# Fixed places in VectorE's queue for joins, combining and turned rows, and earlier pair sums, in a float32 encoder block with Strassen-like products

## The chip, the core and the metric

The kernel runs on one NeuronCore of one Trainium2 chip. The metric is the device time of one execution in microseconds. A core has five engines that run side by side and meet only at semaphores: TensorE (PE, the matmuls; PEld are its weight loads), VectorE (DVE), ScalarE (ACT), GpSimd (POOL) and SyncE (SP, which here issues the DMAs that bring weights in). TensorE writes its results into PSUM, eight banks in all; the kernel hands PSUM out in four tiles of two banks.

## What is computed

One layer of an encoder block on 256 rows of 2048 float32 values: half a SwiGLU feed-forward step, a mixer (causal pooling and gated linear attention), cross-attention to 256 memory rows, and a second feed-forward half step. Of the reference only this matters here:

```python
def swiglu(h, w_gate, w_up, w_down):
    return (jax.nn.silu(h @ w_gate) * (h @ w_up)) @ w_down

x = x + 0.5 * swiglu(rms_norm(x, ffn1_norm), ffn1_w_gate, ffn1_w_up, ffn1_w_down)
...                                   # mixer and cross-attention, which the change does not touch
x = x + 0.5 * swiglu(rms_norm(x, ffn2_norm), ffn2_w_gate, ffn2_w_up, ffn2_w_down)
out = rms_norm(x, final_norm)
```

The hidden width is 5632 = 11 x 512 columns.

## The kernel before, in words

**Precision by splitting.** Every float32 matrix is split into a high part (ScalarE: a copy rounded to fp32r, `wh`, `xh`) and a low part (VectorE: the source less the high part, `wl`, `xl`). A product is then three matmuls: high x high, high x low, low x high (`products`, L330).

**Weights' units.** All weights come in units of 1 MB (`raw`, 128 x 2048). A unit is loaded by one DMA, split, and multiplied. `Stream` (class at the head of the file) keeps a list of units and, between them, operations (`st.op(f, after)`: f is placed after so many further units). `emit` walks the list and splits weights two units ahead of the one being multiplied (`AHEAD = 2`; three `raw` buffers, three buffers each of `wh` and `wl`).

**Two kinds of units.** A plain unit (called p below) covers two k-tiles by 1024 columns: one high copy of 128 x 2048 on ScalarE, one low part of 128 x 2048 on VectorE (L248), 24 matmuls. A seven unit (called s; `split_seven`, `seven`) replaces eight block products by seven, in Winograd's manner: VectorE forms column sums `T` (three additions, L431), then the low part `xl` (128 x 1536, L248) and the low part `wl` of T (L435); ScalarE makes `xh` and two halves of `wh` (L434); TensorE has 21 matmuls (L456). The left operands of a seven unit are sums of pairs of activation tiles, made once for a feed-forward step by `Sums.make` (L387 to L399, four pairs: `x_sums`).

**A block** (`block_s`) is one pass over all 2048 rows of a weight for 1024 columns, in the order s0 p1 s2 p3 s4 s6 p5 p7. It uses all four PSUM tiles. Two hold the parts that only seven units feed (banks P1, P6 and P7, P5); the other two hold P2, P4 (called j=1) and P3, P0 (j=0). After the last seven unit, `combine` (L512 on ScalarE, L513, L514, L517 on VectorE) folds the first two tiles into an SBUF tile `sg` and so frees them. After p7, `join` (L527, twice: j=1, then j=0) adds the other two tiles to `sg` and frees those. The first unit of the next block first multiplies into its P1, P6, P7, P5 (12 matmuls) and then into P2, P4, P3.

**A feed-forward step** has its hidden columns in three parts of 4, 4 and 3 x 512 (`FF_PARTS`). Parts one and two run the blocks G1 (gate), U1 (up), G2, U2 and then the product with w_down. Part three runs G1, U1, one block `both` for the remaining gate and up columns, and w_down. The very first G1 of a step has no seven units (`block_t`); meanwhile `x_sums` is made. I call the change from U1 to G2 the early seam and that from G2 to U2 the late seam. After U1, `late_up` (L787) multiplies gate by up, and `turn` transposes the hidden rows into `ys` in the middle of the next block: 16 transposes into two PSUM tiles named `ph` (L797), a high copy on ScalarE (L253) and a low part on VectorE (L254). `CLEAR = 7` puts this after seven units of the next block, that is between its p5 and p7.

**What sets the order.** The program is not issued as written: a planner reorders the instructions of each engine by its own model of their times and by priorities, and hands out PSUM tiles as they come free in that plan. Only edges restrain it. `in_turn` chains every operation of the weights' splitting on VectorE and on ScalarE into one sequence. `among_weights(f)` inserts f's instructions into these two sequences: behind the newest splitting operation, ahead of the next. `behind_weights(f)` only keeps f behind. In the kernel before, `combine` in the feed-forward steps, `x_sums.make` and a few more are among the weights; `join` and the split in `turn` are not, so the planner puts them where it likes.

Of the kernel before, what the change touches and what calls it, by code (L numbers as in the profile page):

```python
# [90 lines left out]
def build(ctx, tc, I, out):  # L91
    nc = tc.nc
    st = Stream()
# [70 lines left out]
    sums = ctl("sums", [P, 2])  # L164
# [73 lines left out]
    def among_weights(f):  # L238


        scalar, vector = behind_weights(f)
        latest["vector"] = vector
        if scalar is not None:
            latest["scalar"] = scalar
# [7 lines left out]
    def split(hi, lo, src):  # L252
        high = nc.scalar.copy(hi, src)  # L253
        return high, nc.vector.tensor_tensor(out=lo, in0=src, in1=f32(hi), op=ALU.subtract)  # L254
# [202 lines left out]
                    banks[n], x, w, start=n in fresh and j == 0, stop=n in ends and j == 2  # L457
                )

    def block_s(srcs, act, sums, order, evict, merge=None, sevens=None):  # L460

        sevens = [g for g in order if g in (sevens or sums.pairs)]
        held, seen = {"banks": {}}, set()

        def banks(*names):
            t = ptile(uid("pt"))
            for i, n in enumerate(names):
                held["banks"][n] = t[:, i]  # L470
            return t

        def open_whole():
            if "ps" not in held:
                c = banks("P2", "P4")
                held["ps"] = (banks("P3", "P0"), c)

        def open_parts():
            held["parts"] = (banks("P1", "P6"), banks("P7", "P5"))

        names = {(1, 0): "P2", (1, 1): "P4", (0, 0): "P3", (0, 1): "P0"}

        def unit_s(g):
            def fn(weights):
                if g == sevens[0]:
                    open_parts()
                open_whole()
                fresh = {f"P{i}" for i in range(1, 8)} - seen
                seen.update(fresh)
                ends = ("P1", "P5", "P6", "P7") if g == sevens[-1] else ()  # L490
                seven(held["banks"], act, sums, g, fresh, ends, weights)
            return fn

        def unit_p(g):
            def fn(wh, wl):
                open_whole()
                wh, wl = (w.rearrange("p (k j n) -> p k j n", j=2, n=NB) for w in (wh, wl))
                for j in (1, 0):
                    for h in range(2):
                        n = names[j, h]  # L500
                        for kk in range(2):
                            products(held["banks"][n], act, 2 * g + kk, h, wh[:, kk, j],
                                     wl[:, kk, j], n not in seen and kk == 0,
                                     g == order[-1] and kk == 1)
                        seen.add(n)
            return fn

        def combine():

            e = held["e"] = scope["pool"].tile([P, 4, NB], F32, tag="sg", name=uid("sg"), bufs=2)  # L510
            a, b = held["parts"]
            nc.scalar.copy(e[:, 0], a[:, 0])  # L512
            nc.vector.tensor_tensor(out=e[:, 3], in0=a[:, 1], in1=e[:, 0], op=ALU.add)  # L513
            nc.vector.tensor_tensor(  # L514
                out=e[:, 1:3], in0=b, in1=e[:, 3:4].to_broadcast([P, 2, NB]), op=ALU.add
            )
            last = nc.vector.tensor_tensor(out=e[:, 3], in0=b[:, 1], in1=e[:, 1], op=ALU.add)  # L517
            if merge is not None:
                merge(e[:, 2:4], e[:, 0:2])
            return None, last  # L520

        def join(j):
            if merge is not None:
                evict(j, held["ps"][j])
                return
            e = held["e"][:, 0:2] if j else held["e"][:, 2:4]
            nc.vector.tensor_tensor(  # L527
                out=e, in0=held["ps"][j], in1=e, op=ALU.add if j else ALU.subtract
            )
            evict(j, e)  # L530

        for g in order:
            if g in sevens:
                st.unit(srcs[g], unit_s(g), split_seven)
                if g == sevens[-1]:
                    st.op(combine if merge else lambda: among_weights(combine))
            else:
                st.unit(srcs[g], unit_p(g))
        for j in (1, 0):
            st.op(lambda j=j: join(j))  # L540
# [35 lines left out]
    def wwide(w, n0, k0=0, nk=KT):  # L576

        def src(k):
            def load(raw):
                raw = raw.rearrange("p (k n) -> p k n", n=2 * NB)  # L580
                if len(loaded) < 3:
                    for kk in range(2):
                        parts = (0, NB) if not loaded else (0,)
                        for c in parts:
                            n = 2 * NB // len(parts)
                            wload(raw[:, kk : kk + 1, c : c + n], w, k + kk, 1, n0 + c, n)
                else:
                    wload(raw, w, k, 2, n0, 2 * NB)
                next(first_loads, None)
                loaded.append(1)  # L590
            return load
        return [src(k0 + k) for k in range(0, nk, 2)]
# [171 lines left out]
    def ffn(wg, wu, wd, down, amid=None):  # L764
        gate = {}
        x_sums = Sums("xe", xs, PAIRS, True)

        def hidden():
            e = scope["pool"].tile([P, 4, NB], F32, tag="sg", name=uid("sg"), bufs=2)
            return {0: e[:, 2:4], 1: e[:, 0:2]}  # L770

        def ev_gate(j, c, fresh):

            if fresh and fresh == 1 + j:
                gate["new"] = hidden()
            g = gate["new"][j] if fresh else c
            gate[j] = g
            for h in range(2):
                nc.scalar.activation(g[:, h, :], c[:, h, :], AF.Silu, scale=Rcol[:, h : h + 1])

        def late_up(held, j, c):
            behind_weights(lambda: ev_up(j, c, held))

        def ev_up(j, c, held=gate):
            g = held[j]
            for h in range(2):
                nc.vector.scalar_tensor_tensor(  # L787
                    out=g[:, h, :], in0=c[:, h, :], scalar=Rcol[:, h : h + 1], in1=g[:, h, :],
                    op0=ALU.mult, op1=ALU.mult,
                )  # L790

        def turn(g, k):

            v = four(ptile(uid("ph")))
            for i in range(4):
                for h in range(2):
                    nc.tensor.transpose(  # L797
                        v[:, i, h * P : (h + 1) * P], g[:, h, i * P : (i + 1) * P], ident
                    )
            split(ys[:, k : k + 4, 0, :], ys[:, k : k + 4, 1, :], v)  # L800

        for i, g in enumerate(PAIRS):
            st.op(lambda g=g: among_weights(lambda: x_sums.make(g)), (4, 7, 9, 10)[i])
        for lo, n in FF_PARTS:
            whole = n == KT // 4
            for b in range(0, n - 1, 2):
                n0 = (lo + b) * NB
                if lo == b == 0:
                    block_t(wwide(wg, n0), xs, lambda j, ps: ev_gate(j, ps, 1), amid=amid)
                else:  # L810
                    block_s(wwide(wg, n0), xs, x_sums, ORDER, lambda j, c: ev_gate(j, c, 0))
                held, up = {}, {}
                into_down = whole and b
                block_s(wwide(wu, n0), xs, x_sums, ORDER, up.__setitem__)
                st.op(lambda held=held: held.update(gate))
                for j in (1, 0):
                    st.op(lambda j=j, held=held, up=up: late_up(held, j, up[j]),
                          0 if into_down else 3)
                wait = 1 if into_down else CLEAR
                for j in range(2):  # L820
                    st.op(lambda j=j, b=b, held=held: turn(held[j], 4 * (b + j)), wait)
            if n % 2:
                def both(j, c):
                    if j:
                        ev_gate(1, c, 0)
                        gate[0] = gate[1]
                    else:
                        ev_up(0, c)
                block_s(wtwo(wu, wg, (lo + n - 1) * NB), xs, x_sums, ORDER, both)
                st.op(lambda n=n: turn(gate[0], 4 * (n - 1)), 1)  # L830
            if whole:
                make_y_sums()
            down(wd, 4 * lo, 4 * n, lo + n == FF // NB, y_sums if whole else None)
# [646 lines left out]
```

## Time and profile before

| what | us |
|---|---|
| median of 3 runs before (2124.1 to 2125.37) | 2124.6 |
| the profiled execution, its own time | 2124.74 |
| span of its trace, first to last instruction | 2122.9 |
| TensorE busy | 2095.6 |
| VectorE busy | 1705.0 |
| ScalarE busy | 1108.7 |
| DMA queues busy, share of 16 engines | 61% |
| granted TensorE clock, mean | 0.995 |

The rows quoted below have these forms. A timeline row: start, duration (us from the span's start), engine, line, operation, tile written <- tiles read, shapes, count, and in brackets the idle time of the engine ahead of it and what ended it. A row of the waits: who waited for whom, us in total, times, longest. A row of the chain (followed back from the last instruction): start, us, what. A row of the windows: the stretch, its length, then for PE, PEld, DVE, ACT and POOL the busy time and count, the granted clock, the DMA share and GB/s. Matmuls are pipelined: one of 512 columns shows about 0.39 us, while the next starts about 0.227 us after it.

### The profile page before, as it was taken

The numbers are of one execution on the slowest core, as the hardware profiler recorded it, in microseconds if no ns is written. First come the engines' busy times: TensorE is split into PE (matmuls) and PEld (weight loads), VectorE is DVE, ScalarE is ACT, GpSimd is POOL, SyncE is SP. The second block draws the span as 40 slices with busy tenths as digits, with TensorE's granted clock in tenths as the row PEclk, the third lists the DMA queues.
The fourth block names the chain that finished last, engine by engine and source line by source line (L and its number), as shares of the span: only waits on it lengthen the run. The fifth ranks groups of instructions, "written<-read, shape, count | busy, mean of one in ns | idle before, by whom it ended". The sixth has DMA issues, their size and how long they took to land.

```text
span 2122.9 us, 24500 instructions
## 1 busy us (share of the span) xinstructions
PE 2095.6 (99%) x9916; PEld 1748.2 (82%) x9916; DVE 1705.0 (80%) x1537; ACT 1108.7 (52%) x1084; POOL 14.3 (1%) x41
## 2 busy tenths in 40 slices
PE   9999999999999999999999999999999999999998
PEld 8778888788888888888888888888788887888876
DVE  6998899988997577688765546779988999889974
ACT  7554455544554545454645434456554555445544
POOL 0000000000000000000000000000000000000001
PEclk9999999999999999999999999999999999999999
DMA  7556666566656565467755555665567655676673
GB/s 268 187 196 213 246 204 208 185 218 237 218 198 241 198 199 181 157 198 243 252 179 175 163 172 165 198 231 185 198 218 236 220 190 191 214 242 213 201 256 118
DMA packets 143609, 435.95 MB, mean 205 GB/s; under 512 B 9860, under 2 KB 13544, under 8 KB 143112
## 3 DMA queue, kind: packets, MB, share of 16 engines
q1 hardware_dynamic: 143464, 434.38, 61.2%
q8 instruction: 78, 1.28, 0.2%
q14 instruction: 35, 0.29, 0.0%
q10 hardware_dynamic: 32, 0.01, 0.0%
HBM read 417.58 MB, written 16.78 MB: 205 GB/s over the span
## 4 chain that ended last, share of the span: by engine, by line
PE 82%; DVE 13%; issue 2%; ACT 1%; DMA 1%; SPq 0%; DVEq 0%; ACTq 0%
PE pt L330 39%; PE pt L456 15%; PE pa L315 15%; PE pb L330 6%; DVE wl L248 3%; PE pe L330 3%; DVE T L431 3%; DVE wl L435 2%; DVE xl L248 2%; DVE sg L527 1%; DVE sg L787 1%; PE pl L1215 1%; PE pv L1250 1%; PE ph L797 0%; PE px L718 0%
## 5 line engine op out<-in xcount | busy, mean ns | idle before, releaser
L248 DVE TENSOR_TENSOR wl<-raw,wh 128x2048 fp32r<-128x2048 f32 (+2 forms) x284 | 638.1, 2251 | 286.2 <-ACT wh L247 284.9
L247 ACT CAST wh<-raw 128x2048 fp32r<-128x2048 f32 (+2 forms) x284 | 532.6, 1880 | 408.4 <-PE pt L330 183.1
L330 PE MATMUL pt<-wh,xs 128*128 128x512 f32 x1536 | 495.0, 390 | 0.0
L330 PE MATMUL pt<-wh,ys 128*128 128x512 f32 x1440 | 449.2, 390 | 0.0
L434 ACT CAST wh<-T 128x1024 fp32r<-128x1024 f32 x196 | 205.7, 1053 | 331.2 <-DVE T L431 301.2
L330 PEld LDWEIGHTS pt<-wh,xs 128*128 128x128 f32 x1536 | 287.9, 188 | 59.3
L330 PEld LDWEIGHTS pt<-wh,ys 128*128 128x128 f32 x1440 | 269.9, 188 | 56.0 <-ACT wh L247 0.5
L315 PE MATMUL pa<-xs,wh 128*128 128x512 f32 x896 | 315.8, 397 | 0.0
L330 PE MATMUL pt<-wl,xs 128*128 128x512 f32 x768 | 300.0, 391 | 0.0
L330 PE MATMUL pt<-wl,ys 128*128 128x512 f32 x720 | 280.5, 390 | 0.0
L315 PE MATMUL pa<-xs,wl 128*128 128x256 f32 x896 | 248.3, 281 | 0.0
L435 DVE TENSOR_TENSOR wl<-T,wh 128x2048 fp32r<-128x2048 f32 x98 | 223.8, 2284 | 2.1 <-ACT wh L434 1.8
L315 PEld LDWEIGHTS pa<-xs,wh 128*128 128x128 f32 x896 | 167.6, 188 | 38.1 <-issue 0.3
L248 DVE TENSOR_TENSOR xl<-raw,xh 128x1536 fp32r<-128x1536 f32 x98 | 171.6, 1751 | 12.9 <-ACT xh L247 12.9
L315 PEld LDWEIGHTS pa<-xs,wl 128*128 128x128 f32 x896 | 169.1, 189 | 1.7 <-issue 0.2
L330 PEld LDWEIGHTS pt<-wl,xs 128*128 128x128 f32 x768 | 144.3, 188 | 30.0
L247 ACT CAST xh<-raw 128x1536 fp32r<-128x1536 f32 x98 | 144.9, 1479 | 27.7 <-PE pt L456 22.6
L330 PEld LDWEIGHTS pt<-wl,ys 128*128 128x128 f32 x720 | 135.2, 188 | 28.0
L431 DVE TENSOR_TENSOR T<-T,raw 128x512 f32<-128x512 f32 x196 | 135.3, 690 | 5.3
L456 PE MATMUL pt<-wh,xs 128*128 128x512 f32 x320 | 126.8, 396 | 7.6 <-DVE sg L527 7.6
L456 PE MATMUL pt<-wh,xe 128*128 128x512 f32 x320 | 124.6, 395 | 0.0
L456 PE MATMUL pt<-xh,xs 128*128 128x512 f32 x320 | 120.4, 396 | 2.5 <-DVE sg L527 2.5
(236 smaller groups left out, 2354.1 us busy)
## 6 DMA issues: line engine op xcount, KB each, us to landing
raw<-in_ffn_w_down SPq DMA_DIRECT2D x88, 1024.0 KB, 5.6
raw<-in_ffn_w_up SPq DMA_DIRECT2D x80, 1024.0 KB, 5.0
raw<-in_ffn_w_gate SPq DMA_DIRECT2D x77, 1024.0 KB, 5.0
raw<-in_w_in SPq DMA_DIRECT2D x32, 1024.0 KB, 5.2
raw<-in_xattn_w_kv SPq DMA_DIRECT2D x32, 1024.0 KB, 5.3
raw<-in_w_out SPq DMA_DIRECT2D x16, 1024.0 KB, 5.7
raw<-in_xattn_w_q SPq DMA_DIRECT2D x16, 1024.0 KB, 6.0
raw<-in_xattn_w_o SPq DMA_DIRECT2D x16, 1024.0 KB, 5.6
```

Source lines behind the costliest of these rows:

```text
L247: in_turn("scalar", lambda: nc.scalar.copy(hi, src))
L248: in_turn("vector", lambda: nc.vector.tensor_tensor(out=lo, in0=src, in1=f32(hi), op=ALU.subtract))
L315: nc.tensor.matmul(o, w, x, start=k == 0 and i == 0, stop=last and i == 1)
L330: nc.tensor.matmul(ps, a, w, start=first and i == 0, stop=last and i == 2)
L431: in_turn("vector", lambda: nc.vector.tensor_tensor(out=o, in0=a, in1=b, op=ALU.add))
L434: in_turn("scalar", lambda: nc.scalar.copy(th[:, c], t[:, c]))
L435: in_turn("vector", lambda: nc.vector.tensor_tensor(out=tl, in0=t, in1=f32(th), op=ALU.subtract))
L456: nc.tensor.matmul(banks[n], x, w, start=n in fresh and j == 0, stop=n in ends and j == 2)
L527: nc.vector.tensor_tensor(out=e, in0=held["ps"][j], in1=e, op=ALU.add if j else ALU.subtract)
L787: nc.vector.scalar_tensor_tensor(out=g[:, h, :], in0=c[:, h, :], scalar=Rcol[:, h : h + 1], in1=g[:, h, :], op0=ALU.mult, op1=ALU.mult,)
L1215: nc.tensor.matmul(ps[:, t, :M], ys[:, 4 * h + d, a, tok], xa["K"][:, d, b, :], start=i == 0, stop=i == 11,)
L1250: nc.tensor.matmul(ps[:, d, :S], xa["V"][:, m, a, col], xa["PT"][:, m, b, :], start=i == 0, stop=i == 5,)
```

## The change

Four edits, all about order; no instruction is added or removed.

1. `join` in the feed-forward blocks goes through `among_weights`: both joins of a block stand behind the low part of the next block's p1, and ahead of everything of its s2.
2. `combine` of the up blocks comes one unit later (`late=1`): behind the split of the next block's first unit (s0) instead of behind p7's.
3. The split of turned rows, where `turn` runs inside the next block (all b = 0), goes through `among_weights`: ScalarE's two copies and VectorE's two low parts stand behind s0's split and ahead of p1's.
4. `x_sums.make` for the four pairs comes after units 2, 4, 6, 8 of the first gate block instead of 4, 7, 9, 10.

```diff
-    def block_s(srcs, act, sums, order, evict, merge=None, sevens=None):
+    def block_s(srcs, act, sums, order, evict, merge=None, sevens=None, late=0):
...
-            nc.vector.tensor_tensor(
+            among_weights(lambda: (None, nc.vector.tensor_tensor(
                 out=e, in0=held["ps"][j], in1=e, op=ALU.add if j else ALU.subtract
-            )
+            )))
             evict(j, e)
...
-                    st.op(combine if merge else lambda: among_weights(combine))
+                    st.op(combine if merge else lambda: among_weights(combine), late)
...
-        def turn(g, k):
+        def turn(g, k, queued=False):
...
-            split(ys[:, k : k + 4, 0, :], ys[:, k : k + 4, 1, :], v)
+            parts = lambda: split(ys[:, k : k + 4, 0, :], ys[:, k : k + 4, 1, :], v)
+            among_weights(parts) if queued else parts()
...
-            st.op(lambda g=g: among_weights(lambda: x_sums.make(g)), (4, 7, 9, 10)[i])
+            st.op(lambda g=g: among_weights(lambda: x_sums.make(g)), (2, 4, 6, 8)[i])
...
-                block_s(wwide(wu, n0), xs, x_sums, ORDER, up.__setitem__)
+                block_s(wwide(wu, n0), xs, x_sums, ORDER, up.__setitem__, late=1)
...
-                    st.op(lambda j=j, b=b, held=held: turn(held[j], 4 * (b + j)), wait)
+                    st.op(lambda j=j, b=b, held=held, queued=not into_down: turn(
+                        held[j], 4 * (b + j), queued), wait)
```

## The prediction

> **What bounds the kernel now.** First the head of the page:
>
> ```profile
> span 2122.9 us, 24500 instructions
> PE 2095.6 (99%) x9916; PEld 1748.2 (82%) x9916; DVE 1705.0 (80%) x1537; ACT 1108.7 (52%) x1084; POOL 14.3 (1%) x41
> ```
>
> TensorE is the bound, and no edit takes work from it. A gain can only be time in which it stands. I therefore read what PE waited for over the whole span (the two largest rows), then in 740:1400 us, mixer and attention (last row):
>
> ```profile
> PE pt L456 <- DVE sg L527: 10.0, 4, 2.5
> PE pt L456 <- DVE xl L248: 4.5, 9, 1.4
> PE pt L456 <- DVE xl L248: 0.7, 2, 0.3
> ```
>
> Four times TensorE waits for a join and seven times (nine less two) in the feed-forward steps for a low part `xl`. One more wait, 1.4 for a turned row at the last w_down, has its row below. A matmul's shown end lies 0.16 us behind its slot (0.39 in the rows below, while the next starts after 0.23), so each wait costs 0.16 more than shown: joins 10.6, `xl` 3.8 + 7 x 0.16 = 4.9, turned row 1.6. Next, in the chain, what follows the four joins:
>
> ```profile
> 143.67 6.42 PE pt L456 x20
> 402.49 4.84 PE pt L456 x13
> 407.32 2.75 PE pt L330 x12
> 1535.42 4.83 PE pt L456 x13
> 1792.53 4.74 PE pt L456 x13
> ```
>
> Twelve matmuls in 2.75 us are 0.229 each; at that pace 20 take 4.6 and 13 take 3.0. After each wait TensorE runs slow for a while and loses another 6.42 - 4.6 = 1.8, and 1.8 to 1.9 at the others as well. The four places, all late seams, cost 10.6 + 7.3 = 17.9. With the `xl` waits and the turned row, **24.4 us** can go at most.
>
> Now the second late seam, VectorE's timeline, then rows of ScalarE's and TensorE's:
>
> ```profile
> 396.75 1.22 DVE L527 TENSOR_TENSOR sg<-pt,sg 128x1024 f32<-128x1024 f32 x1
> 397.89 2.28 DVE L248 TENSOR_TENSOR wl<-raw,wh 128x2048 fp32r<-128x2048 f32 x1
> 400.08 1.21 DVE L431 TENSOR_TENSOR T<-raw 128x1024 f32<-128x1024 f32 x1
> 401.22 1.21 DVE L527 TENSOR_TENSOR sg<-pt,sg 128x1024 f32<-128x1024 f32 x1
> 402.36 2.34 DVE L254 TENSOR_TENSOR ys<-ph,ys 128x1024 fp32r<-128x1024 f32 x2
> ```
> ```profile
> 393.95 1.91 ACT L247 CAST wh<-raw 128x2048 fp32r<-128x2048 f32 x1
> ...
> 397.14 1.91 ACT L253 CAST ys<-ph 128x1024 fp32r<-128x1024 f32 x2
> ```
> ```profile
> 392.88 1.03 PE L797 MATMUL ph<-ident,sg 128*128 128x128 f32 x8
> 394.21 1.04 PE L797 MATMUL ph<-ident,sg 128*128 128x128 f32 x8
> 397.85 0.39 PE L330 MATMUL pt<-wh,xs 128*128 128x512 f32 x1
> 399.57 0.40 PE L456 MATMUL pt<-xh,xs 128*128 128x512 f32 x1
> 402.49 0.50 PE L456 MATMUL pt<-wh,xs 128*128 128x512 f32 x1 [2.52 <-DVE sg L527]
> ```
>
> G2 ends at 398.08 (397.85 + 0.23). U2 gets six matmuls into the tile that join j=1 freed, one more, and stands: all else needs a tile that join j=0 (to 402.4) or the turned rows (to 404.7) still hold. The first addition for s2 (400.08) went ahead of both. VectorE has no slack here, but soon after (windows: PE, PEld, DVE, ACT, POOL):
>
> ```profile
> 357.00:402.00 45.00, 42.65 (x194) 34.41 (x192) 44.66 (x36) 25.54 (x22) 0.00 (x0) 1.00 0.58 190
> 425.00:436.00 11.00, 11.00 (x51) 9.09 (x50) 7.48 (x7) 4.75 (x4) 0.00 (x0) 1.00 0.71 254
> ```
>
> Up to 402 it is busy 44.66 of 45; from 425 on it idles 3.5 of 11. So the order decides at the seam, and lost time isn't owed to VectorE afterwards.
>
> **The change part by part.** *Late seams (edits 1 and 3).* Places for VectorE: s0's parts, two turned rows, p1's part, join j=1, join j=0, s2. Steps from the starts above: 1.14 for a 1024-wide operation (396.75 to 397.89), 2.19 for a 2048-wide one (397.89 to 400.08). From 396.75, where s0's last part lets VectorE go: turned rows done 397.89 and 399.03, p1's part 401.22, joins 402.36 and 403.50, then s2. Is ScalarE ready? Its two copies (1.91 together, 0.95 each) come after s0's last high copy, which ends where p1's now starts (393.95), and after the transposes (to 393.91 and 395.25): done 394.9 and 396.2; p1's high copy, 1.8 us, by 398.0, ahead of 399.03. TensorE: PSUM tiles now come free at 397.89, 399.03, 402.36 and 403.50. It multiplies 12 times from 398.08 to 400.8, once more to 401.0, and waits 1.35 for 402.36. Does it run slow after that?
>
> ```profile
> 82.04 0.50 PE L456 MATMUL pt<-xl,xs 128*128 128x512 f32 x1 [1.36 <-DVE xl L248]
> 82.38 0.39 PE L456 MATMUL pt<-xh,xs 128*128 128x512 f32 x1
> ```
>
> After 1.5 us the next matmul starts 0.34 later and keeps its pace: no. So 1.35 instead of 2.7 + 1.8 = 4.5.
>
> [...]
>
> *Early seams (edits 1 and 2).* In part two:
>
> ```profile
> 344.41 0.69 DVE L513 TENSOR_TENSOR sg<-pt,sg 128x512 f32<-128x512 f32 x1 [0.64 <-ACT sg L512]
> 347.00 1.22 DVE L431 TENSOR_TENSOR T<-raw 128x1024 f32<-128x1024 f32 x1
> 349.59 1.75 DVE L248 TENSOR_TENSOR xl<-raw,xh 128x1536 fp32r<-128x1536 f32 x1
> 352.40 1.23 DVE L527 TENSOR_TENSOR sg<-pt,sg 128x1024 f32<-128x1024 f32 x1 [1.06 <-PE pt L330]
> ```
>
> Both waits sit where VectorE holds parts that it could make. With s0's parts put first, from 343.76 (344.41 - 0.64): additions 2.6 (347.00 to 349.59), `xl` 1.7, `wl` 2.2 to 350.3; `combine` 2.6 to 352.9, p1's part to 355.1, joins to 356.2 and 357.4. TensorE starts G2 at 354.69, needs the first tiles then (352.9) and the others 2.7 later, at 357.4: just covered. If the cover were short by x, it would cost x. VectorE enters s2 1.7 earlier than now (359.08). That lead ends the `xl` wait in G2's s6 (0.48) and thins the 1.35 to 0.45, at which ScalarE's chain of copies sets the pace. Between 0.45 and 1.35 I take **1.0 for each late seam**, since a lead has 40 us in which to be lost.
>
> *Pair sums (edit 4).* While the first gate block runs, VectorE waits for high copies: in 8:50 us and in 1417:1435 us (the third row is a window with one pair's making, tile `j`: DVE, ACT)
>
> ```profile
> DVE wl L248 <- ACT wh L247: 6.2, 4, 3.3
> DVE wl L248 <- ACT wh L247: 5.1, 3, 2.5
> 63.60:68.58 4.98, 2.61 (x7) 0.81 (x2) 1.00 0.45 179
> ```
>
> One pair is 2.6 us on VectorE. One pair more moves out of U1 into these gaps; another leaves its middle for its start. VectorE comes about 2.4 ahead at U1's s6, where the 1.5 of 82.04 goes. In exchange s0 and its seams get tighter in part one of the first step: I count 0.3 at U1's start, 0.6 for join j=1 at its early seam, 0.6 at G2's s6. In the second step, which has more gaps, nothing.
>
> *Third parts.* Their seam leads into w_down:
>
> ```profile
> 2046.77 0.50 PE L330 MATMUL pe<-wh,ys 128*128 128x512 f32 x1 [1.43 <-DVE ys L254]
> 2041.34 1.91 ACT L247 CAST wh<-raw 128x2048 fp32r<-128x2048 f32 x1 [5.16 <-DMA raw<-in_ffn_w_down]
> 2043.15 1.92 ACT L253 CAST ys<-ph 128x1024 fp32r<-128x1024 f32 x2
> ```
>
> The turned rows stood behind a copy that a DMA held up. In their new places they come ahead of it; the 1.6 goes. DMAs move with the release of `raw`, by less than 3 us, and queue past nothing new.
>
> **The sum.** Left standing: late seams 4 x 1.0, part one of the first step 1.5. Gone: 24.4 - 5.5 = 18.9. The profiled execution took 2124.74, 0.14 above the median: 2124.7 - 18.9 = **2106**. Its own range: all gone, 2100; 2 us left at each late seam and half of the `xl` waits, 2112.
>
> **The rivals.**
>
> *The wait only moves on (partial).* If the lead is lost and U2 waits again for its s2 or s6, each late seam saves half: 2124.7 - 4 x 2.2 - 1.6 = 2114. For it: 44.66 of 45. Against it: 3.5 idle of 11.
>
> *The first tiles of U2 are not those of the turned rows.* If PSUM tiles went round in a fixed turn, U2 would begin on join j=1's tile: from 398.08 to 402.36, a wait of 4.3 with 1.8 of slowness, 1.6 worse than now at four seams; less 4.9 and 1.6 from the other waits: about 2125. At the first late seam
>
> ```profile
> 146.82 0.53 PE L456 MATMUL pt<-wh,xs 128*128 128x512 f32 x1
> 144.67 1.21 DVE L254 TENSOR_TENSOR ys<-ph,ys 128x1024 fp32r<-128x1024 f32 x1
> 145.80 1.21 DVE L527 TENSOR_TENSOR sg<-pt,sg 128x1024 f32<-128x1024 f32 x1
> ```
>
> the second tile was in use at 146.82, when the turned row had ended (145.88) and the join had not (147.01): handed out as it came free. That speaks against it.
>
> *Slower: a turned row blocks the queues.* Now the parts of p1, both joins and all of s2 stand behind L254 on VectorE, and p1's high copy behind L253 on ScalarE. If the planner puts the transposes at G2's very end instead of 392.88, they end at 400.1, the copies at 401.1, turned rows at 402.4, p1's high copy at 403.0, its part at 405.2, the joins at 406.3 and 407.5. TensorE stands 401.3 - 400.1, then from 404.0 to 406.3, with 1.8 of slowness, and loses about 6.5 with the transposes' 2.0 counted as now: 2 more than today. Four late seams +8; the third parts, with no slack for their first tiles, +2 instead of -1.6; the rest -3: 2131. It decides once the second copy ends after 396.9, from where each us late costs one per seam; at 3 us late nothing is won. For it: now these copies run 2 us after their transposes. Against it: this delay was ScalarE doing p1's and s2's copies first, which the edges forbid, and the transposes stood in G2's last third.
>
> [...]
>
> **How the numbers follow.** Forecast (2100 to 2112) 0.60; the wait moves on (2112 to 2120) 0.09; slowness that does not hang on the waits (2113) 0.03; tiles in turn (about 2125) 0.10; blocked queues (2127 to 2135) 0.18. 0.2% is 4.2 us, about what a measurement can tell from no change. Faster, below 2120.4: 0.72; within: 0.10; slower: 0.18. The range leaves out the blocked queues alone: 2100 to 2127.
>
> **What would show it.** Right: no PE row behind L527 over 1.4 us, no slow matmuls at the late seams; on VectorE two L254 rows, one L248, two L527 in this order; `xl` waits below 1.5 us in all; no PE wait for L254 at w_down. Wrong: U2's first matmul released by L527 (tiles in turn), VectorE idle ahead of L254 (blocked), new PE waits for `xl` or `wl` in U2 (moved on), or for L513 and L517 at early seams (`combine` too late).

## The result, and the profile after

The changed kernel takes **2102.18 us** (median of 4 runs, 2101.99 to 2102.72) beside 2124.35 for the kernel before in the same comparison (2122.75 to 2125.37): 22.2 us less, a ratio of 0.9897 with a 95% interval of 0.988 to 0.9914. A later comparison gave 2101.77 beside 2123.94. The head of the page, and what TensorE waited for over the whole span (waiting <- releasing, us in total, times, longest):

```profile
span 2100.2 us, 24513 instructions
PE 2085.5 (99%) x9916; PEld 1743.5 (83%) x9916; DVE 1704.1 (81%) x1537; ACT 1108.3 (53%) x1084; POOL 14.1 (1%) x41
```
```profile
PE pt L456 <- DVE sg L527: 1.6, 4, 1.0
...
PE pt L456 <- DVE xl L248: 0.7, 2, 0.3
```

No engine's work has changed (the 13 more instructions are waits for semaphores). The four waits for joins have shrunk from 10.0 to 1.6, the nine for `xl` from 4.5 to 0.7 (the two left are those of mixer and attention), and the row for the turned row at w_down is gone. Second late seam, VectorE, then ScalarE and TensorE:

```profile
389.19 2.35 DVE L254 TENSOR_TENSOR ys<-ph,ys 128x1024 fp32r<-128x1024 f32 x2
391.69 2.29 DVE L248 TENSOR_TENSOR wl<-raw,wh 128x2048 fp32r<-128x2048 f32 x1 [0.16 <-ACT wh L247]
393.90 2.35 DVE L527 TENSOR_TENSOR sg<-pt,sg 128x1024 f32<-128x1024 f32 x2
396.17 1.22 DVE L431 TENSOR_TENSOR T<-raw 128x1024 f32<-128x1024 f32 x1
```
```profile
389.75 1.91 ACT L247 CAST wh<-raw 128x2048 fp32r<-128x2048 f32 x1
```
```profile
391.63 0.39 PE L456 MATMUL pt<-xh,xs 128*128 128x512 f32 x1
...
394.59 0.39 PE L456 MATMUL pt<-wh,xe 128*128 128x512 f32 x1
395.18 0.50 PE L456 MATMUL pt<-xh,xs 128*128 128x512 f32 x1 [0.20 <-DVE sg L527]
395.51 0.39 PE L456 MATMUL pt<-xl,xs 128*128 128x512 f32 x1
```

This is the sequence that the prediction wrote down: two turned rows, one part of p1, two joins, then s2. U2 starts at 391.63, when the second turned row has just left VectorE (389.19 + 2.35 = 391.54), and issues 13 matmuls (391.63 to 394.59). The fourteenth comes 0.59 after the thirteenth instead of 0.23, so TensorE stands 0.36 us, and the next matmul follows after 0.33. In the chain of waits (start, us, what), what follows the six matmuls behind that wait:

```profile
396.83 2.72 PE pt L330 x12
```

Twelve matmuls in 2.72 us are 0.227 each, and the rows above keep the same pace: no slow matmuls. The windows shown of before, moved 6.4 us forward because U2 starts at 391.63 instead of 398.08:

```profile
350.60:395.60 45.00, 44.80 (x205) 36.68 (x204) 44.50 (x36) 24.31 (x20) 0.00 (x0) 1.00 0.55 189
418.60:429.60 11.00, 11.00 (x50) 9.09 (x50) 8.56 (x6) 5.38 (x4) 0.00 (x0) 1.00 0.77 279
```

VectorE is as full up to the seam as before (44.50 of 45) and still idles behind it (2.4 of 11 us). The time was not won by making it faster: TensorE's count in the first stretch goes from 194 to 205 with the same VectorE.

Below, "stands" is how much later than 0.227 us a matmul starts after the one before it, summed where several do; at the feed-forward seams that is 1.20 at 142.5, 0.36 at 395.2, 0.35 at 1522.8 and 0.36 at 1775.3 (late), and 0.27 at 98.1 (early): **2.5 us in all**, where the prediction left 5.5 of 24.4. 24.4 - 2.5 = 21.9 of the 22.7 by which the spans differ. The rest is small delays that come with a wait (the matmul behind it starts 0.11 us late), at fewer places. The start of the kernel takes 0.1 longer (the first seven unit begins at 54.12 instead of 54.00).

### The profile page after: what moved, and what is told of

It reads as the page before. It is cut to its first block, busy times and chain, and to the rows that moved or that the text cites. A ratio compares the mean times of both kernels' runs of the same rounds, so it can differ in the third digit from the quotient of the medians.

```text
span 2100.2 us, 24513 instructions
## 1 busy us (share of the span) xinstructions
PE 2085.5 (99%) x9916; PEld 1743.5 (83%) x9916; DVE 1704.1 (81%) x1537; ACT 1108.3 (53%) x1084; POOL 14.1 (1%) x41
## 4 chain that ended last, share of the span: by engine, by line
PE 93%; DVE 4%; issue 1%; ACT 1%; DMA 0%; SPq 0%; DVEq 0%
PE pt L330 45%; PE pt L456 20%; PE pa L315 15%; PE pb L330 6%; PE pe L330 3%; DVE T L431 1%; PE ph L797 1%; DVE wl L248 1%; DVE wl L435 1%; DVE xl L248 1%; PE pl L1217 1%; PE pv L1252 1%; PE px L718 0%; ACT wh L247 0%; DVE sg L527 0%
## 5 line engine op out<-in xcount | busy, mean ns | idle before, releaser
L247 ACT CAST xh<-raw 128x1536 fp32r<-128x1536 f32 x98 | 145.0, 1479 | 21.9 <-PE pt L456 16.5
```

Source lines behind the costliest of these rows:

```text
L247: in_turn("scalar", lambda: nc.scalar.copy(hi, src))
```

## The experiments

The theory at the outset: TensorE stands at the late seams because VectorE makes other things before it frees PSUM, and places for the turned rows and the joins end that; slow matmuls follow only a long wait. Rivals: one of the four edits carries the whole gain, and the slowness has another cause.

### One edit at a time, and two

First only the joins' places (the other three edits undone):

```diff
-            among_weights(parts) if queued else parts()
+            parts()
-            st.op(lambda g=g: among_weights(lambda: x_sums.make(g)), (2, 4, 6, 8)[i])
+            st.op(lambda g=g: among_weights(lambda: x_sums.make(g)), (4, 7, 9, 10)[i])
-                block_s(wwide(wu, n0), xs, x_sums, ORDER, up.__setitem__, late=1)
+                block_s(wwide(wu, n0), xs, x_sums, ORDER, up.__setitem__)
```

> Only edit 1: the joins stand behind p1's part; combine, turned rows and pair sums as before. Theory (what TensorE waits for at a late seam is the order in which the four PSUM tiles come free): tiles now come free at about 400.1 and 401.2 (joins), then the turned rows, so the wait at a late seam is about 2.0 us instead of 2.7 and the slowness may stay; at the early seams of the first parts, where VectorE has no lead, about 1 us and 0.6 us of new waits for a join; the xl waits (4.9) and the 1.6 at the last w_down stay. About 2116 us, 8 us faster than before. Rival (the joins' places alone are the cause): within 3 us of the full change, 2102 to 2105.

Measured: 2114.8 us (2113.03 to 2115.99) beside 2123.89, 9.1 less, ratio 0.9957 [0.9942, 0.9972]. VectorE and TensorE at the second late seam:

```profile
397.94 2.35 DVE L527 TENSOR_TENSOR sg<-pt,sg 128x1024 f32<-128x1024 f32 x2
400.21 1.21 DVE L431 TENSOR_TENSOR T<-raw 128x1024 f32<-128x1024 f32 x1
401.34 2.34 DVE L254 TENSOR_TENSOR ys<-ph,ys 128x1024 fp32r<-128x1024 f32 x2
```
```profile
399.31 0.47 PE L456 MATMUL pt<-xh,xs 128*128 128x512 f32 x1 [1.70 <-DVE sg L527]
```

The joins now come ahead of s2 and of the turned rows, but the turned rows hold two PSUM tiles until 403.7, so U2 starts on what a join frees and stands 1.86. At the first seam of each step it stands 2.19 and 2.20, with slow matmuls behind (3.9 in all each), and at two early seams the joins bring new waits of 1.0 and 0.47. With small delays counted, 12.5 of the 17.9 us of the four late seams stay. Another 3.4 us and more comes from the `xl` waits, which were expected to stay: of the seven only the first, 1.5, is left (the row's other two are those of mixer and attention).

```profile
PE pt L456 <- DVE xl L248: 2.0, 3, 1.3
```

Only the turned rows' places (edits 1, 2 and 4 undone in the same way):

```diff
-            among_weights(lambda: (None, nc.vector.tensor_tensor(
+            nc.vector.tensor_tensor(
                 out=e, in0=held["ps"][j], in1=e, op=ALU.add if j else ALU.subtract
-            )))
+            )
```

> Only edit 3: the split of the turned rows stands behind s0's split and ahead of p1's; joins, combine and pair sums as before. Theory: the two tiles that come free first at a late seam are those of the turned rows, so U2 begins without a wait and the waits at late seams shrink to about 1 us each, without slow matmuls; xl waits (4.9) stay, the 1.6 at the last w_down goes. About 2109 us, 15 us faster than before. Rival (joins are the cause): less than 4 us faster, 2121 or more.

Measured: 2107.16 us (2106.74 to 2107.88), 16.7 less, ratio 0.9922 [0.9907, 0.9937]. TensorE's waits, then VectorE at the second late seam:

```profile
PE pt L456 <- DVE xl L248: 4.6, 9, 1.4
```
```profile
394.35 1.22 DVE L254 TENSOR_TENSOR ys<-ph,ys 128x1024 fp32r<-128x1024 f32 x1
395.49 1.21 DVE L527 TENSOR_TENSOR sg<-pt,sg 128x1024 f32<-128x1024 f32 x1
396.62 1.22 DVE L254 TENSOR_TENSOR ys<-ph,ys 128x1024 fp32r<-128x1024 f32 x1
397.75 1.21 DVE L527 TENSOR_TENSOR sg<-pt,sg 128x1024 f32<-128x1024 f32 x1
398.88 2.28 DVE L248 TENSOR_TENSOR wl<-raw,wh 128x2048 fp32r<-128x2048 f32 x1
```

No row for joins is left, and no slow matmul; of the late seams only the first stands, 0.64 for a turned row. The planner, free to place the joins, puts them between the turned rows and ahead of p1's part, which is better than the place that edit 1 gives them. All seven `xl` waits stay. So **this one edit ends nearly all of the four late seams, and the wait at w_down**. By the starts of the matmuls, small delays counted, the four seams go from 17.9 us to 1.5 and w_down from 1.7 to nothing, while the kernel's start takes 1.2 longer (a wait for `x`): 16.9 us, as much as the spans (2122.9 and 2106.0) differ.

Both together (edits 1 and 3):

> Edits 1 and 3 without the lead that edits 2 and 4 give VectorE. Theory: 1.35 us left at each late seam, xl waits (4.9) stay, new waits for join j=1 of about 1.1 and 0.6 us at the early seams of the first parts; the 1.6 at the last w_down goes. 24.4 - 12 = 12.4 us faster: 2112 us. Rival (the lead does nothing; the places do it all): 2102 to 2104.

Measured: 2107.77 us (2107.18 to 2108.49), ratio 0.9925 [0.9909, 0.9942]: no gain on the turned rows alone, and 4 us better than expected. One row of TensorE's waits:

```profile
PE pt L456 <- DVE xl L248: 2.1, 3, 1.4
```

Joins ahead of all of s2 leave 0.84 to 1.21 at each late seam and 0.94 and 0.47 at early seams; in return VectorE gains a lead, and of the seven `xl` waits only the first, 1.5 in part one's U1, stays (the row's other two are those of mixer and attention). That they would go was the miss.

Only the sooner pair sums (edit 4):

> Only edit 4: pair sums after units 2, 4, 6, 8. Theory: VectorE comes 2.4 to 2.9 us ahead in the first parts; the xl waits there go (1.5, 1.0, 0.5). At the first step's late seam TensorE comes as much earlier as VectorE, so the wait for the join stays; at the second step's it shrinks from 4.4 to under 1.5. The second parts and third parts are as before. 3 to 7 us faster: 2117 to 2121. Rival (VectorE's load in the first part was the whole of it): 2110 or less.

Measured: 2117.93 us (8 runs, 2115.94 to 2119.72), 6.0 less, ratio 0.9972 [0.9962, 0.9983]. The wait for `xl` in the first U1 (1.53 at 82.0 before) is gone, the one at 124 falls from 1.0 to 0.47. The late seams stay, three with slow matmuls behind 2.7 us; the third stands 2.33, where under 1.5 was expected, and has none:

```profile
1528.77 0.39 PE L456 MATMUL pt<-xh,xs 128*128 128x512 f32 x1
1531.32 0.50 PE L456 MATMUL pt<-wh,xs 128*128 128x512 f32 x1 [2.17 <-DVE sg L527]
1531.66 0.39 PE L456 MATMUL pt<-wl,xs 128*128 128x512 f32 x1
```

The next starts after 0.34, and those behind it go on at 0.23.

### One edit undone

Without the joins' places (edits 2, 3 and 4):

> The change without edit 1 (joins left to the planner; edits 2, 3, 4 stay). Theory: the turned rows' places free U2's first two tiles and that is enough; the joins behind p1's part are themselves what is left at the seams of the changed kernel (2.5 us in four late and one early seam), so these go, while VectorE may again wait for a join at early seams and leave an xl wait of 0.5 in the parts two and three. 2100 to 2103 us. Rival (joins need their places, or the planner puts them late again): 2107 or more.

Measured: **2099.57 us** (2099.28 to 2099.86) beside 2122.88, ratio 0.9889 [0.9873, 0.9906]. VectorE at the first early seam and at the second late one, then ScalarE and TensorE at the early one:

```profile
96.32 1.22 DVE L431 TENSOR_TENSOR T<-raw 128x1024 f32<-128x1024 f32 x1
97.46 2.35 DVE L527 TENSOR_TENSOR sg<-pt,sg 128x1024 f32<-128x1024 f32 x2
...
391.08 1.22 DVE L527 TENSOR_TENSOR sg<-pt,sg 128x1024 f32<-128x1024 f32 x1
392.21 2.28 DVE L248 TENSOR_TENSOR wl<-raw,wh 128x2048 fp32r<-128x2048 f32 x1
```
```profile
97.65 1.04 ACT L434 CAST wh<-T 128x1024 fp32r<-128x1024 f32 x1 [5.14 <-DVE T L431]
```
```profile
97.11 0.39 PE L456 MATMUL pt<-wh,xe 128*128 128x512 f32 x1
98.75 0.50 PE L456 MATMUL pt<-wh,xs 128*128 128x512 f32 x1 [1.25 <-ACT wh L434]
```

At the late seams the first join comes ahead of p1's part, and no late seam stands at all. The price is one place, 1.41 at the first early seam: T for s2 went ahead of the joins, the planner put a matmul that needs s2's high copy first in TensorE's sequence, and all behind it wait for that copy. So **edit 1 is no part of the gain; it costs 2.3 at the late seams and saves 1.1 at one early seam** (0.27 instead of 1.41).

Without the later `combine` (edits 1, 3 and 4):

> The change without edit 2. Theory: VectorE loses its 1.7 us of lead in the second parts; the join wait at their late seams grows from 0.36 to about 1.1 and that is nearly all: 2103 to 2105 us. Rival (late combine is idle, or costs at the early seams): 2102 or less.

Measured: 2103.86 us (2103.44 to 2104.12), ratio 0.9909 [0.9894, 0.9924]. VectorE at the early seam of part two, and at the late seam 42 us on:

```profile
339.21 0.69 DVE L513 TENSOR_TENSOR sg<-pt,sg 128x512 f32<-128x512 f32 x1 [1.13 <-ACT sg L512]
...
383.93 1.22 DVE L431 TENSOR_TENSOR T<-raw 128x1024 f32<-128x1024 f32 x1
```

`combine` stands first in the queue and waits 1.13 for ScalarE's copy, which starts at 338.60, when TensorE's last matmul of the seven units (338.12 + 0.39) and ScalarE's own copy of `xh` are done. No wait comes of it at this early seam. But VectorE enters the late seam at 383.93 instead of 382.73, and that seam stands 1.18 instead of 0.36; the third and fourth 0.85 and 0.82 instead of 0.35 and 0.36. Together 1.8 us, beside 1.7 between the medians: the edit's worth is a lead that is spent 40 us later.

Without the sooner pair sums (edits 1, 2 and 3):

> The change without edit 4. Theory: the xl wait of 1.5 in the first step's first U1 comes back, and with VectorE later by 2.4 to 2.9 in the first parts about 1 us at the early and the late seam of each: 2105 to 2108 us. Rival (pair sums do nothing once the places are fixed): 2102 to 2103.

Measured: 2106.26 us (2106.18 to 2106.3), ratio 0.9921 [0.9906, 0.9935], 4.1 above the full change. The `xl` waits in U1 are there again (0.23 and 1.53), the joins' waits at early seams (0.97, 0.46), and the third late seam stands 1.17 instead of 0.35: 3.7 us in all (0.27 of the early seams' was there before).

### The slower rival

Turning behind the whole block instead of after seven units, which brings the transposes to G2's very end:

```diff
-    CLEAR = 7
+    CLEAR = 8
```

> The change with CLEAR = 8: the transposes of turned rows come behind the block's last matmul, the case of my slower rival. Mechanism: the copies on ScalarE and the low parts on VectorE then end 4 us later and p1's part and the joins stand behind them. At a late seam TensorE waits about 1.1 for its first tile and 2.3 for join j=1, 3.4 in all and up to 5.2 with slow matmuls, against 0.6 in the changed kernel; at the third parts 1.1. About 2115 without slowness, 2123 with it; the rival as it was priced before the result says 2131. If places in the queue block nothing: 2102 to 2104.

Measured: 2110.42 us (2109.26 to 2111.3), ratio 0.994 [0.9925, 0.9955], 8 above the changed kernel and between what the two sides expected. The largest row of TensorE's waits, then VectorE at the second late seam:

```profile
PE pt L456 <- DVE ys L254: 6.5, 4, 2.0
```
```profile
389.57 2.28 DVE L248 TENSOR_TENSOR wl<-raw,wh 128x2048 fp32r<-128x2048 f32 x1
392.33 2.35 DVE L254 TENSOR_TENSOR ys<-ph,ys 128x1024 fp32r<-128x1024 f32 x2 [0.48 <-ACT ys L253]
394.60 2.35 DVE L527 TENSOR_TENSOR sg<-pt,sg 128x1024 f32<-128x1024 f32 x2
```

The blocked queue is real: VectorE idles 0.48 ahead of the turned rows, and TensorE stands 1.65 at five seams (three late ones and both third parts) and 2.20 at the first late one: 10.5 us, 8.2 more than the changed kernel's 2.3. Yet TensorE waits there for the turned rows themselves and not for what stands behind them: p1's part (389.57) has moved ahead of them, since the split is now emitted after it; it fills the delay, and nothing turns slow. The rival's own case, late transposes with p1's part still behind them, was not tried.

### How long a wait turns matmuls slow

The changed kernel with 1, 2, 3 and 4 additions of 128 x 512 (0.7 us each, results unused) ahead of the first join at the four late seams; then with 3, 4, 2 and 5:

```diff
+            for _ in range(extra if j else 0):
+                among_weights(lambda: (None, nc.vector.tensor_tensor(
+                    out=jtile().rearrange("p (k s) -> p k s", k=2), in0=f32(xs[:, 0:2, 0, :]),
+                    in1=f32(xs[:, 0:2, 1, :]), op=ALU.add,
+                )))
```

> The change with 1, 2, 3 and 4 extra VectorE additions (128 x 512, about 0.7 us each, results unused) ahead of join j=1 at the four late seams in order of time. Theory: what stands ahead of the join on VectorE costs TensorE its whole time, so waits of about 1.9, 1.8, 2.5 and 3.2 us; slow matmuls (0.43 us apart) follow the long ones and add 1.5 to 1.9 us each, surely from 2.7 us on. About 7 us of waits more and 2 to 4 us of slowness more: 2111 to 2113 us. Rival (VectorE's slack behind the seam hides part of it): under 2107.

> As the dose kernel before, with 3, 4, 2 and 5 additions: waits of about 3.4, 3.2, 1.8 and 4.0 us, slow matmuls after three of them. About 10 us of waits and 5 of slowness more: 2115 to 2118 us. If slowness hung on something else than the length of the wait, the same matmuls would be slow in both dose kernels or in neither.

Measured, one run each: 2112.22 and 2118.41 us. TensorE in the first of the two, second and third late seam (the joins are line 532 here):

```profile
397.74 0.50 PE L456 MATMUL pt<-xh,xs 128*128 128x512 f32 x1 [1.53 <-DVE sg L532]
398.08 0.40 PE L456 MATMUL pt<-xl,xs 128*128 128x512 f32 x1
398.32 0.40 PE L456 MATMUL pt<-xh,xs 128*128 128x512 f32 x1
...
1527.22 0.50 PE L456 MATMUL pt<-xh,xs 128*128 128x512 f32 x1 [2.25 <-DVE sg L532]
1527.56 0.55 PE L456 MATMUL pt<-xl,xs 128*128 128x512 f32 x1
1527.90 0.63 PE L456 MATMUL pt<-xh,xs 128*128 128x512 f32 x1
1528.33 0.63 PE L456 MATMUL pt<-wh,xs 128*128 128x512 f32 x1
```

| additions | wait at the join, us | slow matmuls behind, their cost in us |
|---|---|---|
| 0 (changed kernel) | 0.35 to 1.20 | none |
| 1, 2, 2 | 1.80, 1.69, 1.69 | none |
| 3, 3 | 2.41, 3.23 | yes: 1.6, 1.5 |
| 4, 4 | 3.13, 3.14 | yes: 1.4, 2.7 |
| 5 | 3.85 | yes: 1.6 |

The cost is what the seam loses beyond the wait and beyond the 0.4 us of small delays that the three seams without slow matmuls show too. A slow matmul starts 0.43 us after the one before, 0.2 later than the 0.23 of the others. The slowness came back at the same places, in the same kernel, as soon as the waits were long enough (2.41 us and more), so the short waits are what ended it. The late seams of the second kernel cost 11.9 us of waiting and 5.8 of slowness, 17.7 together and 15.4 more than the changed kernel's 2.3; its time is 16.2 above.

### Joins placed in up blocks only

Both parts of what the kernel without edit 1 taught: the joins' places for the early seams, free joins at the late ones.

```diff
+            add = lambda: nc.vector.tensor_tensor(
                 out=e, in0=held["ps"][j], in1=e, op=ALU.add if j else ALU.subtract
-            )))
+            )
+            among_weights(lambda: (None, add())) if late else add()
```

> The change, but only the joins of up blocks (at early seams) have places; those of gate blocks (at late seams) are the planner's. Theory: places help where the planner guesses VectorE's time wrong (the first early seam, where without places TensorE stood 1.4 us for a high part of s2) and hurt where they put p1's part ahead of join j=1 (late seams, 1.2 + 3 x 0.36 us). Left at the feed-forward seams about 0.3 us: 2098 to 2100 us, at or below the run without any join places (2099.6). Rival (places for joins matter nowhere): 2099.6 again with the 1.4 us wait still there.

Measured: 2099.53 us (2099.34 to 2099.73) beside 2122.48, ratio 0.989 [0.9873, 0.9906].

```profile
PE px L655 <- DMA x<-in_x: 1.4, 1, 1.4
```

The 1.41 is gone and 0.24 is all that stands at any feed-forward seam. The median doesn't show it: it is that of the kernel without edit 1. In this profile TensorE stands 1.4 us at the very start for `x`, which takes back 1.0 of the 1.2. Whether it does so in every run was not settled; this wait varies between 0 and 1.8 in the profiles shown here. The changed kernel once more:

> The changed kernel once more, unaltered, because the kernels without the joins' places at the late seams ran on other chips than it did and came out 2.6 us below it (2099.5 against 2102.2). Theory: the difference is the kernel's own, made of the join waits left at its late seams (1.20 + 0.36 + 0.35 + 0.36 us) and early seam (0.27), so it stands at 2101.7 to 2102.7 again and its waits for the joins at 2.2 to 2.7 by the pace of the matmuls. Rival: the chip makes the difference; then it comes out at 2099 to 2101 beside a kernel before at about 2122.5.

Measured: 2101.77 us (2101.62 to 2101.94) beside 2123.94, ratio 0.9901 [0.9885, 0.9918], with the same waits (1.20, 0.36, 0.36, 0.35 and 0.24). Eight runs of the changed kernel lie between 2101.6 and 2102.7, eight of the two without the joins' places at the late seams between 2099.3 and 2099.9. By these the two are 2.2 to 2.6 us faster than the changed kernel, and their spans say the same (2097.6 and 2097.8 against 2099.8). At the feed-forward seams TensorE stands 1.1 and 2.3 us less in them. But the intervals of the ratios overlap, and they were never compared in the same runs.

## Why the prediction was right, point by point

**The bound and the ceiling** held. 24.4 us was all that could go in the feed-forward steps, and 21.9 went.

**Late seams**: the mechanism was right and two sizes were off. The order, the 13 matmuls without a wait and the end of the slowness came as written. The mis-sized term is "4 x 1.0": it measured 1.20 + 0.36 + 0.35 + 0.36 = 2.3. Between 0.45, where ScalarE's chain sets the pace, and 1.35 the prediction took a value near the upper end, because a lead has 40 us in which to be lost. At three seams it was not lost: p1's part starts on ScalarE's copy (0.16 of idle time at 391.69), the lower end. At the first seam it was. VectorE begins s0 there and at the second late seam at

```profile
130.34 1.22 DVE L431 TENSOR_TENSOR T<-raw 128x1024 f32<-128x1024 f32 x1
...
382.73 1.22 DVE L431 TENSOR_TENSOR T<-raw 128x1024 f32<-128x1024 f32 x1
```
```profile
138.16 0.41 PE L456 MATMUL pt<-xh,xs 128*128 128x512 f32 x1
...
142.53 0.50 PE L456 MATMUL pt<-xh,xs 128*128 128x512 f32 x1 [1.03 <-DVE sg L527]
```

The first U2 starts at 138.16, 7.8 us after VectorE began s0, against 391.63 - 382.73 = 8.9 at the second. Of the 1.1 us that are missing, VectorE makes up about 0.25 (141.26 - 130.34 = 10.9 us to the first join instead of 393.90 - 382.73 = 11.2, where 0.16 goes by waiting for ScalarE); the other 0.84 is the difference between 1.20 and 0.36.

**Which edit does it** the prediction left open by working out edits 1 and 3 as one queue. Edit 3 alone brings 16.7 us. Edit 1 alone brings 9.1, and on top of the others it costs: the joins' places, which the prediction counted into the cause, are not needed for it (2099.57 without them).

**Early seams**: "just covered" was right where the joins are concerned (no wait in part two, 0.27 in part one). The lead came as written: with `combine` in its old place the second late seam stands 1.18, with the late one 0.36, where the prediction had 1.35 and 0.45. But it is not the lead from `combine` alone that ends the `xl` waits in the later blocks: they are gone with the joins' places alone as well, which the prediction didn't see.

**Part one of the first step**: 0.3 + 0.6 + 0.6 was counted as the price of the sooner pair sums; only 0.27 came, at the early seam. The 1.5 at 82.0 went as said, and came back where the pair sums were late again. The gaps in the first gate block bore more than the prediction trusted them to.

**Third parts**: no wait for a turned row at w_down is left, as said.

**The rivals.** Tiles in a fixed turn: U2 began on the turned rows' tiles, so this is out. The wait moves on: no new wait for `xl` or `wl` appeared in U2. Slowness not tied to the waits (2113, which keeps 4 x 1.8 us of it at the late seams): no run shows this term. The changed kernel has no slow matmul there and its clock stays at 1.00 (last section), and with the additions slow matmuls came behind waits of 2.41 us and more. Blocked queues: with late transposes the waits for L254 are there, at 8 us for the whole kernel, where the prediction priced it 25 above its forecast for an order that the planner did not make.

The two sizes together are 5.5 against 2.5, 3.0 us, and the 0.8 of small delays; that is the difference between 2106 and 2102.2.

## What to carry to other kernels

When an engine keeps to its queue's order, as VectorE did in the kernel without edit 2 (1.13 us of standing ahead of `combine`), and is nearly full around a seam (44.50 of 45 us), ask first which buffer's release is needed first behind the seam, and place that one operation; here it was the turned rows, and pinning the joins too took a better choice from the planner. Count a lead as a thing of its own: a wait removed in a queue may show nothing at its own place and most of a microsecond 40 us later (here 0.82, between 1.18 and 0.36). And a wait that is long enough can cost more than itself (here 1.4 to 2.7 us more behind waits of 2.41 us and up), so halving it can bring more than half.

## What the runs showed of the hardware

The slow matmuls stand where the granted clock is 0.50. In the windows the clock is the third number from the end, and behind the length stands the time that PE is busy. First the second late seam of the kernel before, where the matmuls from 403.42 on start 0.43 us apart:

```profile
399.70:403.11 3.41, 0.89 (x5) 0.54 (x4) 3.41 (x4) 2.27 (x4) 0.00 (x0) 1.00 0.50 141
403.11:406.52 3.41, 3.41 (x10) 2.63 (x9) 3.38 (x5) 1.16 (x3) 0.00 (x0) 0.50 0.42 167
```

The clock of that kernel is 0.50 for 3.41 us from 143.70, 403.11, 1536.34 and 1792.34, and TensorE idles 2.48, 2.52, 2.50 and 2.33 in the 3.41 us ahead of each. In the changed kernel the windows show 1.00 for 10 to 2090 us.

From the kernel with the sooner pair sums alone, two of the late seams that stand long:

```profile
397.76:401.17 3.41, 1.45 (x6) 1.24 (x7) 3.41 (x4) 2.38 (x3) 0.00 (x0) 1.00 0.76 229
401.17:404.58 3.41, 3.41 (x9) 2.65 (x8) 3.38 (x4) 1.13 (x2) 0.00 (x0) 0.50 0.19 78
...
1527.57:1530.98 3.41, 1.59 (x8) 0.97 (x6) 3.41 (x3) 2.31 (x4) 0.00 (x0) 1.00 0.37 71
1530.98:1534.39 3.41, 3.07 (x13) 2.55 (x14) 3.38 (x5) 1.62 (x3) 0.00 (x0) 1.00 0.71 269
```

At the second late seam TensorE is idle for 1.96 of the 3.41 us up to 401.17, and the clock is 0.50 for the next 3.41 us. At the third it waits until 1531.32, 1.82 us of it in the first stretch and the rest in the second, and the clock is 1.00 in both.

By the length of the wait alone the edge is blurred: in these runs no wait up to 1.87 was followed by slow matmuls, all of 2.41 and more were; between them 2.19 and 2.20 were (joins' places alone), 2.20 (turning behind the block) and 2.33 (above) were not. What parts these four was not shown. Waits of 2.2 to 2.7 us were followed by slow matmuls at ten places. Behind such a wait five to eight matmuls came at 0.43 us, which cost 1.4 to 1.8 us; once, in the second kernel with additions, it was twelve (403.02 to 408.14, behind a wait of 3.14), and 2.7 us.
